# Gated norms with one folded product of ones, and an earlier logarithm in the last attention norm

## The chip, the cores and the metric

The kernel runs on one NeuronCore of a Trainium2 chip. The metric is the device time of one execution in microseconds (us). TensorE (PE) multiplies, VectorE (DVE), ScalarE (ACT) and GpSimd (POOL) do the elementwise work, and SyncE (SP) and POOL issue most of the DMAs.

## What is computed

One decoder layer on a sequence of 1024 rows of width 1024, in fp32. The input is normed and projected; one head group is differential softmax attention, the other gated linear attention (GLA). Each head's output is normed over its own channels and gated, and both groups go through one output projection, whose result is normed again and added to the input.

```python
h = rms_norm(x, pre_g)
qa, ka, va, ga, qb, kb, vb, gb, gk_low = split_columns(h @ w_in)
oa = diff_attention(qa, ka, va, lam)                  # 8 heads, 128 channels each
oa = rms_norm(oa, subln_g) * (1 - lam_init) * silu(ga)
ob = gla_chunked(qb, kb, vb, log_a)                   # 4 heads, 256 channels each
ob = rms_norm(ob, gla_g) * silu(gb)
y = concatenate([oa, ob]) @ w_out
return x + rms_norm(y, post_g)
```

`rms_norm` divides by the root of the mean of squares over a head's channels, plus 1e-6.

## The kernel before

**Numbers in two parts.** Products are made in fp32r. Nearly every operand is split into a high part (a cast on ACT, names ending in `_hi`) and a low part (the remainder, a subtraction on DVE, names ending in `_lo`), and a product is three matmuls: high with high, high with low, low with high. A matmul has 128 rows of contraction and up to 512 columns.

**First stage, to about 617 us of the trace.** The projection runs in groups of 12 matmuls (`x`, `y` and `z`, a scheme of seven products for each two by two blocks). ACT casts the weights (`w<-w_raw`), DVE subtracts, the results leave PSUM through ACT copies (`s`) and DVE sums (`c`). From about 233 us on, GLA runs between these groups, a step of the generator `gla` for a group or so. It handles 4 heads in two halves of 512 sequence positions, so it makes eight norms, all in this stage.

**A GLA norm.** Channels lie on the partitions, 256 of them as two tiles of 128. ACT squares both (`sqs`), DVE adds them (`sq`, 128x512), and the sum over the partitions is made on PE: a matmul with a matrix of ones (`gms<-sq_hl,ones`). For that `sq` is split in a high part and a low part, `hl[:, 0]` and `hl[:, 1]`, each 128x512, and two matmuls with ones add up in one bank. ACT then takes the logarithm (`r<-gms,eps_t`) and an exponential for the inverse root, and DVE multiplies. Two or three `yield`s lie between the split and the matmuls, so that groups of the projection stand between them on PE.

**Second stage.** Three streams are merged in the written order: scores and softmax (`sc`, `p`), values (`wtr` transposes, `po` products), and the output projection (`ypart`). An attention norm (`attn_norm`) has 128 channels on the partitions, and its squares are folded already: the squares of the upper 64 partitions (`fold`) are added to those of the lower 64, and the high and the low part of the 64x512 sum lie one above the other in one 128x512 tile, so that one matmul with ones suffices (`ms<-sq_hl,ones`).

**The end.** After the last head (half 1 first, then half 0), `seed` copies partial sums of the output projection, which were kept in DRAM, back into PSUM banks by ACT (`yps<-yp`), and PE adds the products of the attention heads 4 to 7 (128 channels each) on top, in the same banks (`yps`). Tiles of the sequence come in the order `ENDS`: 4, 5, 6, 7, 0 and so on. Heads 4 to 6 of the mix come from DRAM and are split by `mix_pair` (`m_hi<-m_raw` on ACT, `m_lo<-m_raw` on DVE) for two tiles at a time. Head 7 is the last one, and comes straight from its norm, through `gate` (`m_hi<-gate`, `m_lo<-gate`, in `last_part`). The last norm of half 1 is the one that tiles 4 to 7 wait for.

**Order.** Matmuls keep the order in which they are written (`mm`, line 142). All other engines' instructions are recorded by one helper (line 66, so almost every row shows L66) and put in order by a scheduler. `tc.issue_after(ins)` makes it issue an instruction only behind another one; `squared_last` keeps such an instruction, the last half's `sq_hl` cast.

Of the kernel before, what the change touches and what calls it, by code (L numbers as in the profile page):

```python
# [9 lines left out]
F32R = mybir.dt.float32r  # L10
AF = mybir.ActivationFunctionType
ALU = mybir.AluOpType
PSUM = bass.MemoryType.PSUM

P = 128
# [5 lines left out]
DA_HEADS = 8  # L21
# [10 lines left out]
def hymba_kernel(  # L32
# [42 lines left out]
    act, dve, pool = Queue(nc.scalar), Queue(nc.vector), Queue(nc.gpsimd)  # L75

    def fp(t):
        return t.bitcast(F32)

    def cols(half):  # L80
        return slice(half * 512, half * 512 + 512)
# [5 lines left out]
    ones = const.tile([P, P], F32R, name="ones")  # L87
# [41 lines left out]
    def bank(i, shape, name):  # L129
        return psum.tile(shape, F32, tag=f"b{i}", name=name)  # L130
# [4 lines left out]
    def take_bank(shape, name):  # L135
        i = free.pop(0)
        return bank(i, shape, name), i
# [3 lines left out]
    def mm(*a, **k):  # L141
        tc.keep_in_program_order(pe.matmul(*a, **k))  # L142
# [32 lines left out]
    kp = ctx.enter_context(tc.tile_pool(name="kp", bufs=1))  # L175
# [6 lines left out]
    def t_c(name, dt=F32):  # L182
        return t2k("c", 4, name, dt)
# [825 lines left out]
    def gla(g):  # L1009

        u = None
        for half in range(2):
# [7 lines left out]
            o = kp.tile([P, 2, 512], F32, tag="ks0", name="go")  # L1020
# [22 lines left out]
            for m in range(2):  # L1043
                kv, ib = take_bank([P, 2, 256], "kv")
                n = half * 4 + 2 * m
# [17 lines left out]
            for m in range(2):  # L1063
                po, ib = take_bank([P, 2, 256], "gpo")
                for i in range(2):
                    c = slice((2 * m + i) * P, (2 * m + i + 1) * P)
                    for t in range(2):
# [3 lines left out]
                            start=True, stop=(us[2 * m + i] is None),  # L1071
# [9 lines left out]
            sqs = kp.tile([P, 2, 512], F32, tag="k1", name="sqs")  # L1081
            for t in range(2):
                act.activation(sqs[:, t], o[:, t], AF.Square)
            sq = t_c("sq")
            dve.tensor_tensor(sq, sqs[:, 0], sqs[:, 1], ALU.add)
            hl = kp.tile([P, 2, 512], F32R, tag="k1", name="sq_hl")
            act.copy(hl[:, 0], sq)
            dve.tensor_tensor(hl[:, 1], sq, fp(hl[:, 0]), ALU.subtract)
            for _ in range(2 if last else 3):
                yield  # L1090
            ms, ib = take_bank([P, 512], "gms")
            for i in range(2):
                mm(ms, ones, hl[:, i], start=(i == 0), stop=(i == 1))
            r = t_c("r")
            act.activation(r, ms, AF.Ln, bias=eps_t, scale=1.0 / 256)
            free.append(ib)
# [71 lines left out]
    def mix_tiles():  # L1168
        n_mix[0] += 1
        return [  # L1170
            hw.tile([P, 8, P], F32R, tag=f"s2_{n}{n_mix[0] % 2}", name=f"m_{n}")
            for n in ("hi", "lo")
        ]
# [176 lines left out]
    def turn(h, half, kts):  # L1350

        pt = tr_bank("wtr", [P, 512])
        n = 0
        for kt in kts:
            for i in blocks_of(kt, half):
                tr(pt[:, n : n + P], w[h, 4 * half + i][:, kt * P : (kt + 1) * P])
                n += P
        hi = smp.tile([P, 512], F32R, tag="wt_hi", name="wt_hi", bufs=3)
        lo = smp.tile([P, 512], F32R, tag="wt_lo", name="wt_lo", bufs=3)
        turned_last[:] = [act.copy(hi[:, :n], pt[:, :n]).ins]  # L1360
        dve.tensor_tensor(lo[:, :n], pt[:, :n], fp(hi[:, :n]), ALU.subtract)
        return hi, lo

    turned_last, squared_last = [], []

    def weigh(po, half, kts, v, wt):

        hi, lo = wt
        n = 0
        for kt in kts:  # L1370
            ns = len(blocks_of(kt, half)) * P
            for i, (a, b) in enumerate(((v[0], hi), (v[1], hi), (v[0], lo))):
                mm(
                    po[:, 512 - ns :], a[:, kt, :], b[:, n : n + ns],
                    start=(kt == 0 and i == 0), stop=(kt >= 4 * half and i == 2),
                    skip_group_check=True,
                )
            n += ns

    def attn_norm(h, half, o):  # L1380
        if h < DA_HEADS - 1:
            gate = smp.tile([P, 512], F32, tag="gate", name="gate", bufs=2)
        else:
            gate = kp.tile([P, 512], F32, tag=("q1", "k1")[half], name="gate")
        with tc.issue_after(qk_load[0]):
            sp.dma_start(gate, g_d[h][:, cols(half)])
        sq = smp.tile([P, 512], F32, tag="r", name="sq", bufs=1)


        hl = smp.tile([P, 512], F32R, tag="sq_hl", name="sq_hl", bufs=1)  # L1390
        fold = smp.tile([P, 512], F32, tag="fold", name="fold", bufs=1)
        act.activation(fold[:64], o[64:], AF.Square)
        ending = h == DA_HEADS - 1 and half
        with tc.issue_after(turned_last[0]) if ending else nullcontext():
            act.activation(sq[:64], o[:64], AF.Square)
        dve.tensor_tensor(sq[:64], sq[:64], fold[:64], ALU.add)
        ins = act.copy(hl[:64], sq[:64]).ins
        if ending:
            squared_last.append(ins)
        dve.tensor_tensor(hl[64:], sq[:64], fp(hl[:64]), ALU.subtract)  # L1400
        if h == DA_HEADS - 1:

            dve.scalar_tensor_tensor(gate, o, sub_g, gate, ALU.mult, ALU.mult)
        for _ in range(4):
            yield 0.0
        n_tr[0] += 1
        ms = bank(TR[n_tr[0] % 2], [P, 512], "ms")
        mm(ms, ones, hl, start=True, stop=True)
        if h == DA_HEADS - 1 and not half:
            opened[TR[n_tr[0] % 2]] = None  # L1410
        r = smp.tile([P, 512], F32, tag="r", name="r", bufs=1)
        act.activation(r, ms, AF.Ln, bias=eps_t, scale=1.0 / P)
        act.activation(r, r, AF.Exp, scale=-0.5)
        if h < DA_HEADS - 1:
            dve.scalar_tensor_tensor(r, o, sub_g, r, ALU.mult, ALU.mult)
            pool.tensor_tensor(gate, r, gate, ALU.mult)
            sp.dma_start(mixd[h * P : (h + 1) * P, cols(half)], gate)
            stored.append(h)
        else:
            dve.tensor_tensor(gate, gate, r, ALU.mult)  # L1420
            last_mix[half] = gate
        yield 0.0

    def all_values():


        AHEAD = 2
        units = [
            (h, half, kts) for h in range(DA_HEADS) for half in (1, 0)
            for kts in [(k,) for k in range(4 * half + 2)] + [(4 * half + 2, 4 * half + 3)]  # L1430
        ]
        vs, os, turned, norms_todo = {0: v_first}, {}, {}, []
        ahead = iter(units)

        def norm_step():
            while norms_todo:
                c = next(norms_todo[0], None)
                if c is not None:
                    return
                norms_todo.pop(0)  # L1440

        for i, (h, half, kts) in enumerate(units):
            last = kts[-1] == 4 * half + 3

            ahead_by = AHEAD if h < DA_HEADS - 1 else AHEAD
            while len(turned) < min(i + 1 + ahead_by, len(units)):
                u = next(ahead)
                if u[2] == (0,):
                    yield lambda: (u[0], 4 * u[1]) in w
                turned[u] = turn(*u)  # L1450
                if u[2][-1] == 4 * u[1] + 3:
                    used.add(u[:2])
                yield 0.4
                norm_step()
            if kts == (0,):
                o = smp.tile([P, 512], F32, tag="o", name="o", bufs=3)
                po = bank(PO, [P, 512], "po")
            weigh(po, half, kts, vs[h], turned[h, half, kts])
            norm_step()
            if last:  # L1460
                act.copy(o, po)
                if half and h + 1 < DA_HEADS:
                    vs[h + 1] = load_v(h + 1)
                norms_todo.append(attn_norm(h, half, o))
            yield 0.6

            if i == 1:
                yield SOON * DA_HEADS * 10.0 / T
        carry = norms_todo[-1]
        while len(norms_todo) > 1:  # L1470
            norm_step()
        next(carry)
        yield 0.0
        yield lambda: (ENDS[2], 0) in ps_d
        early_ends()
        yield from carry
# [135 lines left out]
    def mix_pair(n):  # L1612

        hi, lo = (t.rearrange("p (a b) c -> p a b c", b=4) for t in mix_tiles())
        for i, st in enumerate(ENDS[n : n + 2]):
            raw = load_mix(st, 4, 3)
            with tc.issue_after(squared_last[0]) if squared_last else nullcontext():
                act.copy(hi[:, i, :3], raw[:, :3])
            dve.tensor_tensor(lo[:, i, :3], raw[:, :3], fp(hi[:, i, :3]), ALU.subtract)
            parts_d[st] = hi[:, i], lo[:, i]  # L1620
# [175 lines left out]
```

## Time and profile before

| | |
|---|---|
| median of 3 runs | 965.5 us (965.3 to 965.58) |
| the profiled execution's own time | 964.64 us |
| its span, first to last instruction | 962.9 us |
| mean granted TensorE clock | 0.998 |
| busy: PE, PE weight loads, DVE, ACT, POOL | 99%, 83%, 76%, 63%, 21% |
| matmuls | 4640 |

The page counts an engine as busy while any of its instructions is under way. Matmuls overlap, so the duration of one is longer than the distance to the next, and the busy share of PE doesn't tell how fast they follow one another; the starts in the timeline do. A row of the timeline is: start, duration, engine, line, operation, out<-in, shape, count, and in brackets the idle time of the engine before it and what ended that.

### The profile page before, as it was taken

To read this page: it belongs to the slowest core of one execution; us is meant where nothing else is said; L and a number is where in the kernel's file an instruction comes from. 1 tells how busy PE (TensorE), PEld (TensorE's weight loads), DVE (VectorE), ACT (ScalarE), POOL (GpSimd) and SP (SyncE) were. 2 spreads that over 40 slices of the span, in tenths; PEclk is the share of its full clock that TensorE was granted. 3 is DMA by queue.
4 is the path that set the end of the run, shared out by engine and by line. 5 is a ranking of instruction groups with operands and counts; after the bars stand their busy time and mean duration, and the time that the engine had idled before them with its cause. 6 is when DMAs were issued, how large, how long until landed. Compare 5 with 4: busy or idle time off the path is not lost.

```text
span 962.9 us, 14404 instructions
## 1 busy us (share of the span) xinstructions
PE 953.0 (99%) x4640; PEld 795.9 (83%) x4640; DVE 736.6 (76%) x1468; ACT 603.6 (63%) x1166; POOL 199.0 (21%) x264
## 2 busy tenths in 40 slices
PE   9999999999999999999999999999999999999997
PEld 7887788888888888888888888878888888888875
DVE  5898799996678687687667576587888888898554
ACT  8753355845677556577765344366777787787773
POOL 3101002122142112111100002122222222433321
PEclk9999999999999999999999999999999999999999
DMA  9616367487577897985754498996666669994767
GB/s 343 217 35 167 91 196 253 163 299 246 189 251 239 281 309 236 299 285 193 259 175 145 151 291 273 408 305 198 219 207 208 220 226 357 320 292 104 162 196 149
DMA packets 152827, 220.36 MB, mean 229 GB/s; under 512 B 15728, under 2 KB 85360, under 8 KB 152656
## 3 DMA queue, kind: packets, MB, share of 16 engines
q1 hardware_dynamic: 138304, 177.65, 57.5%
q0 software_dynamic: 14448, 41.79, 14.9%
q8 instruction: 37, 0.61, 0.3%
q14 instruction: 38, 0.31, 0.1%
HBM read 133.93 MB, written 88.60 MB: 231 GB/s over the span
## 4 chain that ended last, share of the span: by engine, by line
PE 96%; ACT 1%; DVE 1%; DMA 1%; issue 0%; SPq 0%; DVEq 0%; ACTq 0%
PE x L142 24%; PE y L142 16%; PE z L142 16%; PE ypart L142 13%; PE sc L142 7%; PE po L142 5%; PE yps L142 4%; PE wtr L145 3%; PE gpo L142 3%; PE kv L142 1%; PE gkl_ps L142 1%; PE pa L142 1%; DMA x<-in_x_dram 1%; PE xT L145 1%; DVE p L66 1%
## 5 line engine op out<-in xcount | busy, mean ns | idle before, releaser
L66 ACT CAST w<-w_raw 128x512 fp32r<-128x512 f32 x138 | 85.2, 621 | 76.8 <-PE y L142 33.6
L66 DVE TENSOR_TENSOR w<-w_raw,w 128x512 fp32r<-128x512 f32 x138 | 94.1, 685 | 38.4 <-ACT w L66 38.2
L66 ACT ACTIVATE p<-p,stt 128x896 f32<-128x896 f32 (+7 forms) x128 | 99.3, 776 | 34.3 <-DVE stt L66 33.0
L66 ACT COPY s<-x 128x512 f32<-128x512 f32 x78 | 44.8, 587 | 74.2 <-PE x L142 74.0
L66 DVE CUSTOM_DVE_ANT_0 p<-sc,maskt 128x512 f32<-128x512 f32 (+3 forms) x128 | 74.3, 585 | 16.0 <-PE sc L142 14.6
L66 POOL TENSOR_SCALAR p<-p,stt,lam 128x1024 f32<-128x1024 f32 (+3 forms) x64 | 56.4, 882 | 144.8 <-DVE stt L66 144.1
L142 PE MATMUL z<-s_hi,w 128*128 128x512 f32 x320 | 80.2, 393 | 0.0
L142 PE MATMUL x<-s_hi,w 128*128 128x512 f32 x320 | 80.1, 392 | 0.0
L142 PE MATMUL y<-h_hi,w 128*128 128x512 f32 x320 | 80.1, 392 | 0.0
L142 PE MATMUL ypart<-wo_hi,m_hi 128*128 128x512 f32 x192 | 79.5, 414 | 0.1
L142 PE MATMUL ypart<-wo_hi,m_lo 128*128 128x512 f32 x192 | 75.5, 393 | 0.0
L142 PE MATMUL ypart<-wo_lo,m_hi 128*128 128x512 f32 x192 | 75.4, 393 | 0.0
L66 POOL DMA_DIRECT2D wo_d<-wo_hi x32 | 17.4, 544 | 275.0 <-ACT wo_hi L66 275.0
L142 PEld LDWEIGHTS z<-s_hi,w 128*128 128x128 f32 x320 | 59.8, 188 | 12.4
L142 PEld LDWEIGHTS x<-s_hi,w 128*128 128x128 f32 x320 | 59.7, 188 | 12.4
L142 PEld LDWEIGHTS y<-h_hi,w 128*128 128x128 f32 x320 | 59.7, 188 | 12.3
L142 PE MATMUL sc<-k,q 128*128 128x512 f32 (+1 forms) x192 | 68.7, 362 | 0.6 <-DVE stt L66 0.6
L142 PE MATMUL sc<-ks,q 128*128 128x512 f32 (+1 forms) x192 | 66.1, 347 | 0.0
L66 ACT CAST wt_hi<-wtr 128x512 fp32r<-128x512 f32 (+1 forms) x80 | 42.8, 535 | 27.1 <-PE wtr L145 26.1
L66 DVE TENSOR_TENSOR wt_lo<-wtr,wt_hi 128x512 fp32r<-128x512 f32 (+1 forms) x80 | 50.6, 632 | 9.0 <-ACT wt_hi L66 8.5
L66 DVE TENSOR_TENSOR w_raw<-w_raw 128x512 f32<-128x512 f32 x80 | 55.2, 690 | 1.2 <-DMA w_raw<-in_w_in_dram 0.2
L66 DVE TENSOR_TENSOR c<-z,s 128x512 f32<-128x512 f32 x48 | 32.8, 687 | 29.8 <-ACT s L66 19.9
(232 smaller groups left out, 2352.0 us busy)
## 6 DMA issues: line engine op xcount, KB each, us to landing
w_raw<-in_w_in_dram SPq DMA_DIRECT2D x40, 512.0 KB, 5.0
wo_d<-wo_hi POOLq DMA_DIRECT2D x32, 256.0 KB, 3.3
q<-q_d SPq DMA_DIRECT2D x32, 256.0 KB, 4.8
k<-k_d SPq DMA_DIRECT2D x32, 256.0 KB, 5.4
ks<-k_d SPq DMA_DIRECT2D x64, 128.0 KB, 5.9
v<-v_d SPq DMA_DIRECT2D x16, 512.0 KB, 6.5
wo_raw<-in_w_out_dram POOLq DMA_DIRECT2D x31, 256.0 KB, 4.8
wo_d<-gqd POOLq DMA_DIRECT2D x22, 256.0 KB, 4.2
```

The costliest lines, as they stand in the source:

```text
L66: ins = op(*a, **k)
L142: tc.keep_in_program_order(pe.matmul(*a, **k))
L145: tc.keep_in_program_order(pe.transpose(dst, src, ident))
```

## The change

Two edits.

In `gla`, the folding of the attention norms is used for the GLA norms too. The upper 64 partitions of `sq` are copied by ACT to the lower partitions of a free tile (`sqs<-sq`, 64x512), DVE adds them to the lower 64 (`sq<-sq,sqs`, 64x512), and the high and low part of the sum, 64x512 each, share one 128x512 tile. One matmul with ones remains of two. For each of the eight norms that is one ACT instruction and one DVE instruction more, and one matmul less.

At the end, the last half of the last head (half 0) copies `o` out of PSUM behind the exponential of half 1's norm, where it stood ahead of that norm's logarithm, and the second tile of the second `mix_pair` call (tile 7, the fourth) is cast behind that exponential too.

```diff
@@ gla
             sq = t_c("sq")
             dve.tensor_tensor(sq, sqs[:, 0], sqs[:, 1], ALU.add)
-            hl = kp.tile([P, 2, 512], F32R, tag="k1", name="sq_hl")
-            act.copy(hl[:, 0], sq)
-            dve.tensor_tensor(hl[:, 1], sq, fp(hl[:, 0]), ALU.subtract)
+            act.copy(sqs[:64, 1], sq[64:])
+            dve.tensor_tensor(sq[:64], sq[:64], sqs[:64, 1], ALU.add)
+            hl = kp.tile([P, 2, 512], F32R, tag="k1", name="sq_hl")[:, 0]
+            act.copy(hl[:64], sq[:64])
+            dve.tensor_tensor(hl[64:], sq[:64], fp(hl[:64]), ALU.subtract)
             for _ in range(2 if last else 3):
                 yield
             ms, ib = take_bank([P, 512], "gms")
-            for i in range(2):
-                mm(ms, ones, hl[:, i], start=(i == 0), stop=(i == 1))
+            mm(ms, ones, hl, start=True, stop=True)
@@ attn_norm
-    def attn_norm(h, half, o):
+    def attn_norm(h, half, o, po):
+        if h == DA_HEADS - 1 and not half:
+            with tc.issue_after(squared_last[1]):
+                act.copy(o, po)
@@
-        act.activation(r, r, AF.Exp, scale=-0.5)
+        ins = act.activation(r, r, AF.Exp, scale=-0.5).ins
+        if ending:
+            squared_last.append(ins)
@@ all_values
-                act.copy(o, po)
+                if i + 1 < len(units):
+                    act.copy(o, po)
@@ mix_pair
-            with tc.issue_after(squared_last[0]) if squared_last else nullcontext():
+            with tc.issue_after(squared_last[i]) if n else nullcontext():
                 act.copy(hi[:, i, :3], raw[:, :3])
```

PE's order is the same in both kernels but for the eight matmuls that are gone. On ACT, at the fifth GLA norm (410 us of the trace; `s` leaves PSUM, `g` is a gate's first step):

```order
 L66 ACTIVATE qk_hi<-c 128x512 x2
 L66 COPY s<-x 128x512
-L66 CAST sq_hl<-sq 128x512
-L66 CAST w<-w_raw 128x512 x2
+L66 COPY sqs<-sq 64x512
+L66 CAST w<-w_raw 128x512 x2
+L66 CAST sq_hl<-sq 64x512
 L66 ACTIVATE g<-c 128x512
 L66 ACTIVATE g<-g 128x512
```

The copy has the cast's old place, and the cast now stands behind two casts of weights. On DVE, at the same norm, the order before:

```order
L66 SCALAR_TENSOR_TENSOR c<-c,qk_hi 128x512 x2
L66 TENSOR_TENSOR sq_hl<-sq,sq_hl 128x512
L66 TENSOR_TENSOR w<-w_raw,w 128x512
L66 TENSOR_TENSOR c<-y,s 128x512
L66 TENSOR_TENSOR w<-w_raw,w 128x512
L66 TENSOR_TENSOR c<-z,s 128x512
```

and after:

```order
L66 SCALAR_TENSOR_TENSOR c<-c,qk_hi 128x512 x2
L66 TENSOR_TENSOR sq<-sq,sqs 64x512
L66 TENSOR_TENSOR w<-w_raw,w 128x512
L66 TENSOR_TENSOR c<-y,s 128x512
L66 TENSOR_TENSOR w<-w_raw,w 128x512
L66 TENSOR_TENSOR sq_hl<-sq,sq_hl 64x512
L66 TENSOR_TENSOR c<-z,s 128x512
```

The sum of the halves has the place of the subtraction, which moves back by four instructions. On ACT at the end (`r` is half 1's logarithm and then its exponential; `fold` and `sq` are half 0's squares), the order before:

```order
L66 CAST m_hi<-m_raw 128x384 x2
L66 COPY yps<-yp 128x512
L66 COPY o<-po 128x512
L66 ACTIVATE r<-ms,eps_t 128x512
L66 ACTIVATE fold<-o 64x512
L66 ACTIVATE r<-r 128x512
L66 ACTIVATE sq<-o 64x512
L66 CAST m_hi<-gate 128x128 x2
```

and after:

```order
L66 CAST m_hi<-m_raw 128x384
L66 ACTIVATE r<-ms,eps_t 128x512
L66 ACTIVATE r<-r 128x512
L66 COPY o<-po 128x512
L66 CAST m_hi<-m_raw 128x384
L66 COPY yps<-yp 128x512
L66 ACTIVATE fold<-o 64x512
L66 ACTIVATE sq<-o 64x512
L66 CAST m_hi<-gate 128x128 x2
```

Three instructions that stood ahead of the logarithm (a cast, the seed `yps` of tile 6 and the copy of `o`) now stand behind the exponential, and `fold` no longer stands between the two. On DVE at the same place:

```order
 L66 TENSOR_TENSOR sq_hl<-sq,sq_hl 64x512
-L66 TENSOR_TENSOR m_lo<-m_raw,m_hi 128x384 x2
+L66 TENSOR_TENSOR m_lo<-m_raw,m_hi 128x384
+L66 TENSOR_TENSOR gate<-gate,r 128x512
 L66 SCALAR_TENSOR_TENSOR gate<-o,sub_g,gate 128x512
-L66 TENSOR_TENSOR gate<-gate,r 128x512
+L66 TENSOR_TENSOR m_lo<-m_raw,m_hi 128x384
 L66 TENSOR_TENSOR sq<-sq,fold 64x512
 L66 TENSOR_TENSOR m_lo<-gate,m_hi 128x128 x2
```

The product of half 1's gate (`gate<-gate,r`) goes ahead of half 0's and of the fourth tile's low part. The scheduler also moves some transfers on SP past one another in the first stage.

More of the change, by code (lines that the diff above doesn't have):

```diff
@@ L1460, in all_values @@
             if last:
-                act.copy(o, po)
+                if i + 1 < len(units):
+                    act.copy(o, po)
                 if half and h + 1 < DA_HEADS:
                     vs[h + 1] = load_v(h + 1)
-                norms_todo.append(attn_norm(h, half, o))
+                norms_todo.append(attn_norm(h, half, o, po))
             yield 0.6
```

## Prediction

> **What bounds the kernel now.** I read the page first, then the stretch of the GLA norms as one window, then the matmuls with ones by tile, and the end engine by engine in the timeline.
>
> ```profile
> PE 953.0 (99%) x4640; PEld 795.9 (83%) x4640; DVE 736.6 (76%) x1468; ACT 603.6 (63%) x1166; POOL 199.0 (21%) x264
> PE 96%; ACT 1%; DVE 1%; DMA 1%; issue 0%; SPq 0%; DVEq 0%; ACTq 0%
> 233.00:617.00 384.00, 384.00 (x1863) 323.85 (x1862) 270.05 (x415) 223.53 (x388) 61.00 (x88) 1.00 0.76 245
> 922.24 34.30 PE yps L142 x151
> ```
>
> The second row is the chain of work that ended last: 96% of it is PE. The third is the window (PE, weight loads, DVE, ACT and POOL busy, then the granted clock and the DMA share): PE has no gap in 384 us, while DVE is busy for 270 and ACT for 224. A matmul taken out there shortens the time, and ACT and DVE work put in is free as long as PE never comes to wait for it. The last row is the chain's final piece: 151 matmuls in 34.30 us, one each 0.227 us, without a stop. So whatever PE gains ahead of 922 us is kept to the end.
>
> **The eight matmuls.** The group of the matmuls with ones, and the fifth norm's pair with its successor:
>
> ```profile
> L142 PE MATMUL gms<-sq_hl,ones x16: 402/403/404, 263.7 to 518.2; 128*128 128x512 f32 x16
> 410.55 0.64 PE L142 MATMUL gms<-sq_hl,ones 128*128 128x512 f32 x2
> 411.03 0.40 PE L142 MATMUL z<-s_hi,w 128*128 128x512 f32 x1
> ```
>
> One takes 403 ns from start to end, but they overlap: the pair starts at 410.55 and the next product at 411.03, so a pair holds PE's order for 0.48 us and one of them for 0.24 us. I take the distance, not the duration: 8 x 0.24 = 1.92 us (by durations it would be 8 x 0.403 = 3.2 us, which the overlap excludes). The Trainium skill (TensorE: Matmul & The Clock Gate, in "Wait — 56ns, not 53.3ns?") gives 215.7 ns from start to start for 512 columns at the full clock; by that the eight would be worth an estimated 1.73 us. The trace's distance is longer, and the sum goes by it.
>
> **What the fold adds.** Per norm one ACT copy and one DVE sum, 64x512, and the cast and the subtraction now handle 64 partitions. Their prices stand in the attention norms, which do the same:
>
> ```profile
> L66 ACT CAST sq_hl<-sq x24: 603/620/632, 256.2 to 918.7; 64x512 fp32r<-64x512 f32 x16, 128x512 fp32r<-128x512 f32 x8
> L66 DVE TENSOR_TENSOR sq_hl<-sq,sq_hl x24: 681/686/1569, 256.9 to 919.4; 64x512 fp32r<-64x512 f32 x16, 128x512 fp32r<-128x512 f32 x8
> ```
>
> Half the partitions take as long: 0.62 us and 0.69 us for either shape, so nothing is saved there. Eight norms add 8 x 0.62 = 5.0 us of ACT and 8 x 0.69 = 5.5 us of DVE, against 160 us in which ACT is idle in that window, and 114 us for DVE. What matters is the chain to the matmul: squares' sum, copy, sum, cast, subtraction, `gms`. It grows by a copy and a sum and by what stands between them, and PE is in strict order: if the tile is late, all that follows is. The shortest margins are at the fifth norm and the eighth:
>
> ```profile
> 369.50 0.68 DVE L66 TENSOR_TENSOR sq_hl<-sq,sq_hl 128x512 fp32r<-128x512 f32 x1
> 373.85 0.40 PE L142 MATMUL gms<-sq_hl,ones 128*128 128x512 f32 x1
> 405.79 0.63 ACT L66 CAST sq_hl<-sq 128x512 fp32r<-128x512 f32 x1
> 408.02 0.63 ACT L66 CAST w<-w_raw 128x512 fp32r<-128x512 f32 x1 [1.10 <-PE y L142]
> 407.42 0.68 DVE L66 TENSOR_TENSOR sq_hl<-sq,sq_hl 128x512 fp32r<-128x512 f32 x1
> 409.22 0.68 DVE L66 TENSOR_TENSOR w<-w_raw,w 128x512 fp32r<-128x512 f32 x1
> 514.72 0.68 DVE L66 TENSOR_TENSOR sq_hl<-sq,sq_hl 128x512 fp32r<-128x512 f32 x1
> 515.32 1.22 DVE L66 TENSOR_TENSOR w<-v_raw,w 128x1024 fp32r<-128x1024 f32 x1
> 518.00 0.64 PE L142 MATMUL gms<-sq_hl,ones 128*128 128x512 f32 x2
> ```
>
> Fifth: the tile was ready at 408.10, 2.45 us ahead of 410.55. In the new order the sum has the place at 407.42, the weights keep 408.02 to 409.90, and the subtraction follows, at about 409.82 to 410.50. ACT's cast, behind the weight cast that begins at 408.02 when PE frees a buffer, is done at about 409.2, in time. What is left is 0.05 us, so a wait of up to 0.1 us is possible; I take 0.05. Eighth: the sum takes the place at 514.72, the weights stay until 516.54, the subtraction ends at about 517.2, 0.8 us ahead of 518.00: no wait. All of this is set off by PE and moves with it. The next shortest margin is the fourth's, from 370.18 to 373.85, 3.7 us, and by the new order its subtraction moves back by three of DVE's instructions, 1.8 us. So the first edit gives 1.92 - 0.05 = 1.87 us, between 1.8 and 1.95. If the cover goes, each microsecond that a tile is late is a microsecond of PE.
>
> **The end.** PE, ACT and DVE between 911 and 920 us:
>
> ```profile
> 912.61 0.50 PE L142 MATMUL ms<-sq_hl,ones 128*128 128x512 f32 x1
> 915.73 0.39 PE L142 MATMUL yps<-wo_hi,m_hi 128*128 128x512 f32 x1
> 917.54 0.39 PE L142 MATMUL yps<-wo_lo,m_hi 128*128 128x512 f32 x1
> 918.23 0.50 PE L142 MATMUL yps<-wo_hi,m_hi 128*128 128x512 f32 x1 [0.30 <-ACT m_hi L66]
> 918.97 0.50 PE L142 MATMUL yps<-wo_hi,m_lo 128*128 128x512 f32 x1 [0.23 <-DVE m_lo L66]
> 919.30 0.40 PE L142 MATMUL yps<-wo_lo,m_hi 128*128 128x512 f32 x1
> ...
> 912.78 0.92 ACT L66 CAST m_hi<-m_raw 128x384 fp32r<-128x384 f32 x2
> 913.61 0.58 ACT L66 COPY yps<-yp 128x512 f32<-128x512 f32 x1
> 914.13 0.57 ACT L66 COPY o<-po 128x512 f32<-128x512 f32 x1
> 914.61 0.68 ACT L66 ACTIVATE r<-ms,eps_t 128x512 f32<-128x512 f32 x1
> 915.97 0.63 ACT L66 ACTIVATE r<-r 128x512 f32<-128x512 f32 x1
> 917.36 0.63 ACT L66 ACTIVATE sq<-o 64x512 f32<-64x512 f32 x1 [0.76 <-DVE gate L66]
> 917.90 0.48 ACT L66 CAST m_hi<-gate 128x128 fp32r<-128x128 f32 x2
> ...
> 916.63 0.69 DVE L66 TENSOR_TENSOR gate<-gate,r 128x512 f32<-128x512 f32 x1 [1.14 <-ACT r L66]
> 918.02 0.68 DVE L66 TENSOR_TENSOR sq<-sq,fold 64x512 f32<-64x512 f32 x1 [0.70 <-ACT sq L66]
> 918.63 0.48 DVE L66 TENSOR_TENSOR m_lo<-gate,m_hi 128x128 fp32r<-128x128 f32 x2
> ...
> 922.96 0.68 ACT L66 ACTIVATE r<-ms,eps_t 128x512 f32<-128x512 f32 x1
> 923.68 0.63 ACT L66 ACTIVATE r<-r 128x512 f32<-128x512 f32 x1
> ```
>
> Here is PE's last stop: from 917.54 to 919.30 three matmuls take 1.76 us where 3 x 0.227 = 0.68 would do, so 1.08 us is lost. PE waits first for the high part of head 7 (`m_hi<-gate`, 917.90), then for its low part (918.63). Both hang on half 1's logarithm, which starts at 914.61 although its sum left PE at 913.11.
>
> In the new order ACT goes on after the first cast (912.78, the next one could begin at 913.2): logarithm 913.20, exponential 0.72 later at 913.92 (as half 0's, 922.96 and 923.68), done at 914.55; `o` from 914.45, cast from 914.93, the seed `yps` 915.35 to 915.93, `fold` from 915.87, `sq` from 916.40, `m_hi<-gate` at 916.94, first one done at about 917.25. On DVE `gate<-gate,r` ends at 915.27, half 0's product at about 915.96, the low part at 916.42, `sq<-sq,fold` runs from 917.06 to 917.74 and `m_lo<-gate` begins at 917.67, first one done by 918.0. Each step is spaced as its like above (0.42 us for a cast of 384 columns, 0.52 for a copy, 0.54 for a square).
>
> What is late next is the seed of tile 6. It ended at 914.19 and ends at 915.93 now, and its first product, the thirteenth matmul behind `ms`, is due at 915.73. PE waits some 0.23 us there. Its nine products end at 918.02; the high part has been there since 917.25, and the low part, needed at 918.25, since 918.0. So 1.08 is lost no more, and 0.23 to 0.3 is lost anew: a gain of 0.8 us. Bounds: 1.08 if the seed is in time, 0.3 if the low part or the seed comes half a microsecond later than worked out. The fourth tile's cast and low part serve tile 7, whose turn comes after those of tiles 4 to 6, and half 0's norm serves tiles 0 to 3, later still; that they move by half a microsecond costs nothing while those turns last.
>
> **Sum.** 1.87 + 0.8 = 2.67 us off the profiled execution's 964.64 us (span 962.9 and 1.74 around it) gives 962.0. The median of the runs, 965.5, is 0.86 above that execution, so the runs should show 962.8. A measurement of this kernel can tell about 0.2%, 1.93 us, from no change: the border is 963.57, and the first edit alone ends almost on it.
>
> **Rivals.**
> - *The end gives nothing* (13%). The seed of tile 6, now behind four more instructions, stops PE for as long as the gate did. For it: my margin there is already negative. Against it: the seed would have to end a full 1.1 us after its turn, at 916.8, and the rows give 915.93. Time: 965.5 - 1.87 = 963.6.
> - *Some of the first edit is given back* (14%). At the fifth norm nothing is left over, and the scheduler has shuffled casts and SP's transfers all over the stage. If the fifth norm's subtraction waits behind one more DVE instruction (0.6 us) and the eighth's behind a wide one (1.22 us, 0.4 past its margin), PE loses 1.0 us: 963.8.
> - *Slower* (5%). The cast `sq_hl` stands on ACT behind casts of weights that wait for PE to free a buffer, as the one at 408.02 does. If that buffer comes free a group of products later than I read it (12 x 0.227 = 2.72 us), the fifth norm loses 2.7 us and the eighth 1.9, which takes all of the 2.67 and 1.9 more: 967.4, and every further norm adds to that. It decides the sign once the eight norms together lose 2.7 us. The rows are against it, as the buffer in question was free at 408.02 in time for the cast. The Trainium skill (TensorE: Matmul & The Clock Gate, in "Architectural detail: the array is 16× 32×32, not 1× 128×128") says that ACT and DVE are strict first-in first-out queues, which is what makes this possible; the trace agrees, with nothing else on ACT begun in the 1.10 us ahead of that cast.
> - *The gain is swallowed later* (4%): a load that is paced by memory rather than by PE, between 617 and 900 us. That stage's PE would then wait where it doesn't now: 965.0.
>
> My forecast has the remaining 64%, 962.3 to 963.4. The range 962.2 to 964.4 reaches from a full 1.08 us at the end over the first rival to the second with some more lost, and leaves out the slower case, the swallowed one and the worst of the second. Faster by over 0.2%: nearly all of my 64%, half of the first rival and a little of the second, 0.73. Slower 0.05. Within 0.2%: 0.22.
>
> **What would show it.** PE should have 4632 matmuls and still no wait between 233 and 617 us, with the fifth `gms` touching its tile's end. The value at 617 should be reached 1.9 us sooner. In the end the logarithm should start within 0.15 us of its sum, a wait for `yps` of 0.2 to 0.3 us should stand before the first product of tile 6, and those for `m_hi` and `m_lo` should be gone. I am wrong if PE waits for `sq_hl` or for weights in the first stage, or if the three waits at the end still add up to a microsecond.

## The result and the profile after

The changed kernel takes 962.55 us (median of 8 runs, 961.8 to 962.77) against 965.4 us for the kernel before on the same chip (8 runs, 964.39 to 966.42). The ratio is 0.9972, with a 95% interval of 0.9964 to 0.9981. The forecast was 962.8 us, faster, and that is what happened: 2.67 us were worked out, and 2.85 are between the medians. That the two lie so close is in part luck: the interval leaves anything from 1.8 to 3.5 us open, the traces give 2.47, and three terms of the first edit's part are off and nearly cancel. One later execution of the changed kernel, at a granted clock of 0.85, took 1054.63 us and is left out of every median and ratio below.

The profiled execution took 962.77 us (span 961.1). Its page line on the engines, the window of the GLA norms (same columns as before), and the last piece of the chain of work that ended last:

```profile
PE 950.8 (99%) x4632; PEld 793.6 (83%) x4632; DVE 741.2 (77%) x1476; ACT 608.9 (63%) x1174; POOL 200.2 (21%) x264
233.00:617.00 384.00, 383.75 (x1861) 323.31 (x1861) 275.53 (x424) 229.45 (x397) 62.22 (x88) 1.00 0.76 246
920.35 34.30 PE yps L142 x151
```

PE has 4632 matmuls, eight fewer. In the window DVE is busy 5.5 us longer than before and ACT 5.9 us, which is the added work (eight instructions each, and one more of either that falls into the window), and PE is no longer quite without a gap: 0.25 us are missing. The last piece is the same 151 products in the same 34.30 us, and it starts 1.89 us earlier than the 922.24 of before, although what comes ahead of the first norm took 0.56 us longer in this execution.

What the weight loads (PEld) waited for between 50 and 616 us (in total, times, longest), in the kernel before and in the changed one. (Not shown is a line on `x`, of the stage ahead of the norms, with 0.2 us before and 0.7 us after.) Then the group of the products of ones in the changed kernel, and its timeline at the two places:

```profile
PEld y L142 <- DVE c L66: 0.3, 1, 0.3
```

```profile
PEld y L142 <- DVE c L66: 0.5, 1, 0.5
PEld gms L142 <- PE z L142: 0.4, 1, 0.4
```

```profile
L142 PE MATMUL gms<-sq_hl,ones x8: 397/397/468, 264.2 to 516.8; 128*128 128x512 f32 x8
```

```profile
409.03 1.07 PE L142 MATMUL z<-s_lo,w 128*128 128x512 f32 x4
410.15 0.47 PE L142 MATMUL gms<-sq_hl,ones 128*128 128x512 f32 x1
410.45 0.86 PE L142 MATMUL z<-s_hi,w 128*128 128x512 f32 x3
...
516.81 0.40 PE L142 MATMUL gms<-sq_hl,ones 128*128 128x512 f32 x1
...
516.82 0.19 PEld L142 LDWEIGHTS y<-w,h_hi 128*128 128x128 f32 x1
517.53 0.53 PEld L142 LDWEIGHTS y<-w,h_hi 128*128 128x128 f32 x3 [0.52 <-DVE c L66]
...
516.78 1.29 DVE L66 TENSOR_TENSOR c<-y,s 128x512 f32<-128x512 f32 x2 [0.74 <-PE y L142]
```

Seven of the eight take 0.40 us, one takes 0.47: the fifth starts at 410.15, though the four products ahead of it, 0.227 apart, would have let it go at 409.94. It and its successor cost PE 0.28 us there. The list of waits names PE's own `z` as the releaser, but the tile of `gms` was finished by DVE only at 410.00, and the load of its weights begins at 410.12; that the tile was the cause is tested below. The eighth goes in time, but the second product behind it comes 0.48 us after the first instead of 0.23: its weights are loaded only at 517.53, when the first of DVE's two `c<-y,s` has read the bank into which that product writes (516.78 to 517.47).

The end, PE first, then ACT and DVE:

```profile
911.43 0.50 PE L142 MATMUL ms<-sq_hl,ones 128*128 128x512 f32 x1
914.32 0.39 PE L142 MATMUL yps<-wo_lo,m_hi 128*128 128x512 f32 x1
914.79 0.50 PE L142 MATMUL yps<-wo_hi,m_hi 128*128 128x512 f32 x1
915.12 0.39 PE L142 MATMUL yps<-wo_hi,m_lo 128*128 128x512 f32 x1
916.96 0.39 PE L142 MATMUL yps<-wo_hi,m_hi 128*128 128x512 f32 x1
917.19 0.40 PE L142 MATMUL yps<-wo_hi,m_lo 128*128 128x512 f32 x1
917.42 0.39 PE L142 MATMUL yps<-wo_lo,m_hi 128*128 128x512 f32 x1
...
912.01 0.68 ACT L66 ACTIVATE r<-ms,eps_t 128x512 f32<-128x512 f32 x1
914.14 0.59 ACT L66 COPY yps<-yp 128x512 f32<-128x512 f32 x1
914.76 0.63 ACT L66 ACTIVATE fold<-o 64x512 f32<-64x512 f32 x1
915.95 0.48 ACT L66 CAST m_hi<-gate 128x128 fp32r<-128x128 f32 x2
...
916.69 0.48 DVE L66 TENSOR_TENSOR m_lo<-gate,m_hi 128x128 fp32r<-128x128 f32 x2
```

The logarithm starts 0.08 us after its sum, the two stops at `m_hi` and `m_lo` are gone (916.96, 917.19, 917.42 without a break), and one stop stands before tile 6's first product at 914.79, which the seed (914.14 to 914.73) holds up by 0.24 us. The product behind it also follows after 0.33 us instead of 0.23, so this stop costs 0.34 us.

### The profile page after: what moved, and what is told of

Same layout as the page of the kernel before. It is cut to its first block, busy times and chain, and to the rows that moved or that the text cites. A ratio compares the mean times of both kernels' runs of the same rounds, so it can differ in the third digit from the quotient of the medians.

```text
span 961.1 us, 14399 instructions
## 1 busy us (share of the span) xinstructions
PE 950.8 (99%) x4632; PEld 793.6 (83%) x4632; DVE 741.2 (77%) x1476; ACT 608.9 (63%) x1174; POOL 200.2 (21%) x264
## 4 chain that ended last, share of the span: by engine, by line
PE 89%; DVE 4%; DMA 3%; SPq 2%; ACT 1%; issue 1%; DVEq 0%; ACTq 0%
PE x L142 21%; PE z L142 15%; PE y L142 14%; PE ypart L142 13%; PE sc L142 7%; PE po L142 5%; PE yps L142 4%; PE wtr L145 3%; PE gpo L142 3%; DMA g_raw<-in_w_in_dram 2%; PE kv L142 1%; DMA ks<-k_d 1%; DVE s_lo L66 1%; PE gkl_ps L142 1%; PE pa L142 1%; DVE s L66 1%
```

## Experiments

No kernel below leaves out any of the work. Most effects are under what a measurement of the total can tell, so the traces are compared by stage, from PE's rows: from three products ahead of the first `gms` to the first `ypart`; from there to the last `ms` but one, half 1's of head 7; from there to PE's last product. In us:

| kernel | norms | middle | end | median of runs | of the kernel before (95%) |
|---|---|---|---|---|---|
| before | 353.57 | 296.05 | 43.92 | | |
| after | 351.81 | 296.07 | 43.21 | 962.55 | 0.9972 (0.9964 to 0.9981) |
| after, again | 351.81 | 296.16 | 43.26 | 962.23 | 0.9977 (0.9967 to 0.9987) |
| first edit alone | 351.84 | 296.05 | 43.91 | 963.33 | 0.9981 (0.9972 to 0.9990) |
| second edit alone | 353.55 | 296.06 | 43.22 | 964.44 | 0.9993 (0.9984 to 1.0002) |
| seed first | 351.78 | 296.06 | 43.18 | 962.55 | 0.9976 (0.9967 to 0.9985) |
| fifth later | 351.51 | 295.16 | 43.26 | 962.11 | 0.9969 (0.9958 to 0.9981) |
| fold in two | 356.19 | 296.08 | 43.22 | 966.53 | 1.0020 (1.0011 to 1.0029) |
| pair at the eighth | 351.79 | 296.08 | 43.22 | 962.42 (one run) | |
| both stops away | 351.51 | 295.15 | 42.84 | 960.64 | 0.9963 (0.9951 to 0.9976) |

Where the order of a stage is the same, two traces agree within 0.11 us. What comes ahead of the first norm is not in the table: it varies from 262.8 to 264.4 us between these traces, and between kernels with the same order there, so the spans alone mislead (the second edit alone has 963.7, the kernel before 962.9).

**The first edit alone.** The norms folded as in the changed kernel, the end as before:

```diff
+            act.copy(sqs[:64, 1], sq[64:])
+            dve.tensor_tensor(sq[:64], sq[:64], sqs[:64, 1], ALU.add)
...
-            for i in range(2):
-                mm(ms, ones, hl[:, i], start=(i == 0), stop=(i == 1))
+            mm(ms, ones, hl, start=True, stop=True)
```

> The kernel before with the first edit alone: eight products of ones, the end as before. My theory, two gains that add up: eight matmuls by 0.24 us less the wait of 0.28 us that the fifth norm shows in the profile after, 1.6 to 1.75 us, so 0.9982 to 0.9984 of the kernel before; in the trace PE stops behind 541 matmuls' worth of the end as before, for m_hi and m_lo, 1.08 us. Rival, the end's new order carries most of it (the first edit is given back in waits or later): under 1.0 us, 0.999 or more, and PE idle between 233 and 900 us where the kernel before had none.

Measured: 1.73 us in the norms' stage, nothing elsewhere, and the end's stops where they were:

```profile
916.92 0.50 PE L142 MATMUL yps<-wo_hi,m_hi 128*128 128x512 f32 x1 [0.30 <-ACT m_hi L66]
917.65 0.50 PE L142 MATMUL yps<-wo_hi,m_lo 128*128 128x512 f32 x1 [0.23 <-DVE m_lo L66]
```

**The second edit alone.** Pairs in the norms, the end in the new order:

```diff
-                act.copy(o, po)
+                if i + 1 < len(units):
+                    act.copy(o, po)
...
-            with tc.issue_after(squared_last[0]) if squared_last else nullcontext():
+            with tc.issue_after(squared_last[i]) if n else nullcontext():
```

> The kernel before with the second edit alone: pairs of products of ones in the GLA norms, the end in the new order. My theory: 0.75 to 0.8 us, 0.9992 of the kernel before, less than what the runs can tell; the trace decides: the waits for m_hi and m_lo at about 918 us are gone, and one of 0.25 us stands before the first product of tile 6. Rival, the end gives nothing alone, because its ACT work is in time only with the rest 1.9 us earlier: 1.000, and the three waits still add up to a microsecond.

Measured: 0.70 us in the end, nothing in the norms. The two parts add up: 1.73 + 0.70 = 2.43, and the changed kernel has 1.76 + 0.71 = 2.47. The rival that one depends on the other is out.

**The seed first.** In the changed kernel, tile 6's seed directly behind the copy of `o`:

```diff
-                seed(ENDS[2], 0, SC[2], sums_of(2)[:, 0])
...
+            if n and i:
+                yp = sums_of(2)
+                with tc.issue_after(squared_last[1]):
+                    seed(ENDS[2], 0, SC[2], yp[:, 0])
...
```

> The changed kernel with tile 6's seed put directly behind the copy of o, ahead of the fourth tile's cast (ACT: logarithm, exponential, o, seed, cast, fold). My theory, the wait of 0.25 us in the end is the seed's place in ACT's order and nothing else: PE goes from ms through tile 6 without a stop, 0.25 us off, 0.9997 of the changed kernel, which the runs can hardly tell and the trace can. Rival, another wait takes its place (the cast now 0.6 us later holds back m_lo, or fold and sq come later and m_hi with them): same time as the changed kernel, a wait of about 0.25 us at m_hi or m_lo.

Measured: 0.03 us. My theory fell and the rival held: tile 6 runs through, and PE stops ten products later for `m_lo`, for the same 0.24 us:

```profile
917.26 0.39 PE L142 MATMUL yps<-wo_hi,m_hi 128*128 128x512 f32 x1
917.72 0.50 PE L142 MATMUL yps<-wo_hi,m_lo 128*128 128x512 f32 x1
...
914.40 0.59 ACT L66 COPY yps<-yp 128x512 f32<-128x512 f32 x1
914.92 0.51 ACT L66 CAST m_hi<-m_raw 128x384 fp32r<-128x384 f32 x1
915.46 0.63 ACT L66 ACTIVATE fold<-o 64x512 f32<-64x512 f32 x1
...
917.39 0.48 DVE L66 TENSOR_TENSOR m_lo<-gate,m_hi 128x128 fp32r<-128x128 f32 x2
```

In the changed kernel the low part starts as late behind `ms` (5.26 us, here 5.29); the stop ahead of it hid that. What sets the time of `m_lo` is ACT's chain: seed, cast, `fold` and `sq` all stand ahead of head 7's parts. The last experiment takes the cast out of it.

**The fifth norm later.** In the changed kernel, the fifth `gms` one group of products later (the next half gives up one of its steps, so that nothing else on PE moves):

```diff
-            yield
+            if (g, half) != (2, 1):
+                yield
...
-            for _ in range(2 if last else 3):
+            for _ in range(2 if last else 4 if (g, half) == (2, 0) else 3):
                 yield
```

> The changed kernel with the fifth norm's product of ones one group of 12 products later in PE's order. My theory, the stop of 0.28 us at the fifth norm is the lateness of its tile and nothing that belongs to a single product of ones: with 2.7 us more of cover the product holds PE's order for 0.47 us as those of the other seven norms, 0.28 us off, 0.9997 of the changed kernel. Rival, the stop belongs to the place (a weight load, or the first product of a group): it stays, or moves along with the product. A few score and softmax instructions at 617 to 650 us move too, which may cost or give some tenths there; so the stage up to 617 us is read by itself.

Measured: the stop is gone, and the product's successor follows after 0.23 us, like the others'. The stage is 0.30 us shorter:

```profile
412.59 0.40 PE L142 MATMUL gms<-sq_hl,ones 128*128 128x512 f32 x1
412.82 0.39 PE L142 MATMUL x<-s_hi,w 128*128 128x512 f32 x1
```

So the stop was the lateness of that one tile. The middle stage is 0.91 us shorter as well, at 630 to 641 us, where score and softmax instructions have moved; which of them did it was not tried.

**The changed kernel again.**

> The changed kernel once more, on the chip of the three below, to compare them with. By its own runs 0.9972 of the kernel before. In its trace the two stops of the first profile stand again if they belong to the order and not to that execution: 0.28 us before the fifth product of ones, and 0.25 us before the second product behind the eighth.

Both stops in the norms stand again, in the same size: the products around the fifth are again 0.28 us late, and the second product behind the eighth again comes 0.48 us after the first. The fifth:

```profile
409.97 0.47 PE L142 MATMUL gms<-sq_hl,ones 128*128 128x512 f32 x1
410.28 1.09 PE L142 MATMUL z<-s_hi,w 128*128 128x512 f32 x4
```

**The fold in two products.** In the changed kernel, the high and the low part side by side on the same 64 partitions:

```diff
...
-            act.copy(hl[:64], sq[:64])
-            dve.tensor_tensor(hl[64:], sq[:64], fp(hl[:64]), ALU.subtract)
...
+            act.copy(hl[:64, 0], sq[:64])
+            dve.tensor_tensor(hl[:64, 1], sq[:64], fp(hl[:64, 0]), ALU.subtract)
...
-            mm(ms, ones, hl, start=True, stop=True)
+            for i in range(2):
+                mm(ms, ones[:64], hl[:64, i], start=(i == 0), stop=(i == 1))
```

> The changed kernel with the folded squares' high and low part in two tiles on the same 64 partitions, so that two products of ones over 64 rows are taken per norm: ACT's and DVE's added work stays, the eight matmuls come back. My theory, what the first edit gives is the matmuls alone, 0.24 us each and some 0.05 by which the ten products behind a pair run slower: six norms give back 0.29, the eighth nothing, and the fifth's stop goes, so 1.5 us more than the changed kernel, about 0.8 under the kernel before (0.9992), all of it from the end. The subtraction now writes the partitions it reads and should start some 0.08 us before the instruction ahead of it ends, not 0.03 behind it. Rival, the gain came from elsewhere (the moved casts and transfers of the stage, a product over 64 rows costing half): the time of the changed kernel, 0.997.

This missed: it is not 0.8 us faster than the kernel before but slower, 1.0020 (1.0011 to 1.0029), and the norms take 4.38 us more than in the changed kernel. The rival is out too. The added ACT and DVE work stays and the gain is gone, as the theory has it, but 4.38 us is not the 1.5 it gave, because a product of 64 rows among products of 128 is dear. So this run can't tell what the eight matmuls alone are worth. Fifth norm of this kernel, weight loads (PEld) and products, and the weight loads there in the kernel before:

```profile
411.83 0.72 PE L142 MATMUL gms<-sq_hl,ones 64*128 64x512 f32 x2
412.49 0.73 PE L142 MATMUL z<-s_hi,w 128*128 128x512 f32 x2
...
411.83 0.29 PEld L142 LDWEIGHTS gms<-sq_hl,ones 64*128 64x128 f32 x2 [0.35 <-ACT g L66]
412.48 0.76 PEld L142 LDWEIGHTS z<-s_hi,w 128*128 128x128 f32 x4 [0.36 <-PE gms L142]
```

```profile
410.32 0.42 PEld L142 LDWEIGHTS gms<-sq_hl,ones 128*128 128x128 f32 x2
```

In the kernel before the pair's weights were loaded from 410.32, while PE was still at the product ahead of 410.55. Here loading begins at 411.83, with the product itself, and again at 412.48 with the first product of 128 rows behind. At each of the eight norms the distances from the product ahead of the pair to the second behind it are 0.32, 0.34, 0.32 and 0.34 us, where 128 rows have 0.23, 0.24, 0.24 and 0.24. The first and the third are the two changes of height, with the late loads; the second and the fourth stand behind a late load, as the 0.335 us behind the late load at the eighth norm of the changed kernel does. The brackets name a releaser, but the distances are the same at all eight norms, with whatever margin the tile was ready. That the change of height is the cause is read from this pattern; no other run has products of 64 rows.

The other half of this expectation came true. The fifth subtraction and the instruction ahead of it, in the changed kernel and in this one:

```profile
408.61 0.67 DVE L66 TENSOR_TENSOR w<-w_raw,w 128x512 fp32r<-128x512 f32 x1
409.32 0.68 DVE L66 TENSOR_TENSOR sq_hl<-sq,sq_hl 64x512 fp32r<-64x512 f32 x1
```

```profile
410.42 0.67 DVE L66 TENSOR_TENSOR w<-w_raw,w 128x512 fp32r<-128x512 f32 x1
411.02 0.68 DVE L66 TENSOR_TENSOR sq_hl<-sq,sq_hl 64x512 fp32r<-64x512 f32 x1
```

Where it writes the upper 64 partitions it starts 0.03 us after the end of `w`, where it stays on the lower ones 0.08 us before.

**The pair at the eighth norm.** In the changed kernel, for the last norm only, unfolded squares and two products:

```diff
+            if last:
...
+                act.copy(hl[:, 0], sq)
+                dve.tensor_tensor(hl[:, 1], sq, fp(hl[:, 0]), ALU.subtract)
...
+            for i, src in enumerate(hl):
+                mm(ms, ones, src, start=(i == 0), stop=(i == len(hl) - 1))
```

> The changed kernel with the pair of products and the unfolded squares of the kernel before at the eighth norm alone. My theory, PE waits there for a bank that DVE's c reads, whatever stands between, so the eighth's second product was free in the kernel before and its removal gave nothing: the stop of 0.25 us behind it goes, the pair takes its place, and from three products ahead of it to ten behind the same work takes the same time within 0.06 us. Rival, a product of ones costs 0.24 to 0.29 us wherever it stands: that stretch is longer by as much, and the stop stays.

Measured: nothing is lost by the ninth product (351.79 against 351.81 us). The rival would have had 352.05 or more. The second product behind the pair now follows the first after 0.23 us, although its weight load still waits 0.28 us for `c`; only the third is late, by 0.11 us:

```profile
516.46 0.64 PE L142 MATMUL gms<-sq_hl,ones 128*128 128x512 f32 x2
516.94 1.88 PE L142 MATMUL y<-w,h_hi 128*128 128x512 f32 x7
...
517.17 1.45 PEld L142 LDWEIGHTS y<-w,h_hi 128*128 128x128 f32 x7 [0.28 <-DVE c L66]
```

**Both stops away.** The fifth norm later, the seed first, and the fourth tile's cast behind head 7's:

```diff
-            with tc.issue_after(squared_last[i]) if n else nullcontext():
...
+            def split(i=i, raw=raw):
                 act.copy(hi[:, i, :3], raw[:, :3])
...
+                late_split.append(split)
...
+            if st == ENDS[1]:
+                with tc.issue_after(act.latest):
+                    late_split[0]()
```

> The changed kernel with both remaining stops of its own taken away: the fifth product of ones one group later, tile 6's seed directly behind the copy of o, and the fourth tile's cast and low part behind head 7's (ACT: logarithm, exponential, o, seed, fold, sq, casts of head 7, fourth tile's cast). My theory, with the cast gone from the chain to m_lo, m_lo comes 0.4 us sooner than it did with the seed first alone, and no wait is left between ms and the end: 0.28 and 0.35 us off, and what the changed score order gives at 630 to 641 us, so 0.6 to 1.5 us under the changed kernel on the same chip. Rival, yet another wait takes the place (tile 7's low part, half 0's squares): the end as with the seed first alone, and the gain of the fifth norm only, 0.3.

Measured: 0.30 us in the norms, 0.37 in the end, 0.92 in the middle. It is the fastest of all, 960.64 us against 962.23 for the changed kernel on the same chip, and 0.9963 (0.9951 to 0.9976) of the kernel before. The two stops are 0.67 us of that; the 0.92 of the middle stage comes with the moved score and softmax instructions, as in the fifth norm later. `m_lo` begins 4.84 us after the start of `ms` (5.26 in the changed kernel), and PE has no stop between `ms` and its end:

```profile
909.65 0.50 PE L142 MATMUL ms<-sq_hl,ones 128*128 128x512 f32 x1
912.50 0.39 PE L142 MATMUL yps<-wo_lo,m_hi 128*128 128x512 f32 x1
912.73 0.40 PE L142 MATMUL yps<-wo_hi,m_hi 128*128 128x512 f32 x1
914.80 0.39 PE L142 MATMUL yps<-wo_hi,m_hi 128*128 128x512 f32 x1
915.03 0.39 PE L142 MATMUL yps<-wo_hi,m_lo 128*128 128x512 f32 x1
...
914.49 0.48 DVE L66 TENSOR_TENSOR m_lo<-gate,m_hi 128x128 fp32r<-128x128 f32 x2
```

## Why the prediction was right, and where it was not

**The bound.** Right. Whatever PE gains ahead of the last 151 products is kept: the middle stage takes 296.05 us before and 296.07 after, the last piece 34.30 in both. The rival of a gain swallowed later is out.

**The eight matmuls, 8 x 0.24 less 0.05, 1.87 us.** The stage gave 1.76, but by other terms. From three products ahead of a `gms` to the sixteenth start behind, PE takes 4.386 us in the kernel before, with the pair in it, and 4.320 in the changed kernel, which in that stretch has got one ordinary product of 0.227 further: a gain of 0.293 per norm. The missing 0.05 is the term that I left out: the ten starts behind a pair are mostly 0.228 to 0.236 apart, and 0.226 to 0.227 from the second behind a single product on. Six norms give 6 x 0.293 = 1.76, which is all of the stage's gain.

**The fifth norm, a wait of 0.05, at most 0.1.** Mis-sized: it lost 0.28 us, which takes all that its matmul was worth. The order of the instructions was as worked out. But I let the subtraction start 0.08 us ahead of the end of `w`, as same-partition instructions do, and it started 0.03 behind; and I let `gms` follow its tile by 0.05, and it took 0.15 (410.00 to 410.15), with another 0.07 at its successor. With a group more of cover the loss is gone. So the step that failed here is the cover that I counted: I gave the tile 0.05 us to spare, and by PE's own pace it was 0.06 us late before any latency.

**The eighth norm, no wait.** Right for the tile, which was ready at 516.05, 0.76 us ahead (0.8 was predicted), and wrong for the norm. The pair of before covered PE's wait for the bank that `c` reads, and half of that cover was removed, so 0.25 us came out as a stop. The experiment with the pair put back shows that the removal gave nothing there. I had asked what the new instructions make late, and not what the removed ones had been hiding. It could have been seen: in the kernel before, the weight load of the same product already waits 0.28 us for `c`, and all that it costs there is 0.1 us at the product behind.

So two norms of eight gave nothing, six gave a fifth more than I took for them, and the sum came out 0.11 short, just under the 1.8 that I had set as its bound. I had written that I am wrong if PE waits for `sq_hl` or for weights in the first stage. It does both, 0.28 us at the fifth norm and 0.25 us at the eighth: the size of this term was nearly right, and the claim that PE would not wait was wrong. The rival that some of this edit is given back was true in kind at these two places, and at neither for the reason that it gave.

**The end, 0.8 us.** Right in mechanism, 0.71 measured. The stop of 1.08 is gone, and the wait for the seed was 0.24 where I had 0.23; the 0.1 at the product behind it makes a loss of 0.34, just beyond the 0.3 that I gave. What I had not seen: head 7's low part was not in time either. In my schedule it began 5.06 us behind the start of `ms` and was ready when due even without the seed's stop, by 0.02 us; it began 5.26 behind, since `fold` started 25 ns behind the end of the seed and `sq` 25 ns behind the end of `fold`, where I had let them overlap (0.07 lost ahead of `fold`, 0.12 behind), and only the seed's stop gave it the time. So 1.08 was not to be had by the seed alone. With 1.76 for the first edit the traces give 2.47 us, 0.2 less than worked out.

**The slower rival.** Out: the ACT cast at the fifth norm stood behind a weight cast as I wrote, and was done at 408.55, 0.7 us before DVE could use it.

## What to carry to other kernels

Before a matmul is taken out, look at what the next products on PE wait for: where a bank or a tile becomes free just in time, the matmul was a cover, and taking it out here gave a stop of the same length (0.25 us for 0.24). One product's price is the distance between starts in the stretch around it, including the slower starts behind it, and not its own distance alone. And where a chain has several links that are all nearly late, curing the one that shows may only move the stop to the next: here the seed and the low part had to be moved together.

## What the runs showed of the hardware

**Partitions and overlap.** In the changed kernel the subtractions that read the lower 64 partitions and write the upper start 31 to 32 ns after the end of the DVE instruction ahead of them, wherever that is busy until then, and the next one 31 to 33 ns after theirs. With both on the lower 64, in the GLA norms of the kernel with the fold in two, the subtraction starts 74 to 83 ns before the end of a busy one ahead. On ACT, `fold<-o` and `sqs<-sq`, which read the upper 64 and write the lower, start 23 to 31 ns behind the end of the one ahead, while the casts `sq_hl<-sq`, on the lower 64 alone, start 94 to 115 ns ahead of it where ACT is busy until then, but for one. The instruction behind `fold` or `sqs` is held too if it reads SBUF (twelve of them start 11 to 26 ns behind the end), and not if it reads PSUM (`wtr`, `ypart`: all six start 94 to 96 ns ahead of the end). So on ACT it is not the crossing alone that counts, but also which memory the neighbour reads.

The Trainium skill (VectorE: DVE Perf Modes, in "Two Vector instructions with no wait between them") says, as a model, that a Vector instruction is held until every earlier one has finished when an input starts in another group of 32 partitions than the first input last read from the same memory, or its output in another than the last one written there. The traces agree, for DVE by the numbers above, and they show the like on ACT, of which that section does not speak. Being held cost the subtraction about 0.1 us at the fifth norm.

**Products over 64 rows.** A pair of products over 64 rows in a stream of products over 128 costs 0.34 us more than a pair over 128. The weights of the first of the pair, and of the first product of 128 rows behind it, are not loaded ahead but with the product itself, and each of these two starts and each start right behind them is about 0.09 us late: 0.32 to 0.34 us from start to start against 0.23 to 0.24. Half the rows saved nothing, and eight pairs of them cost 2.62 us more than eight pairs over 128 (356.19 against 353.57 us in the norms' stage); at the eighth norm the kernel before had a late load of its own.
